# Activations at byte 112 and split weights at byte 176 of every 256, in a decoder trunk on one Trainium2 core

## The chip, the core and the metric

The kernel runs on one core of a Trainium2 chip. The metric is the device time in microseconds (us). Before the change, three timed runs took 594.8, 600.5 and 599.28 us; their median is 599.28 us. The profile is one further execution of the same program.

## What is computed

The reference is a decoder trunk with two layers over 256 tokens and 1024 features. The first layer has causal attention of 16 heads of 64 (one block of 256 keys, so the block selection is empty), the second a windowed attention whose keys and values come from 4 heads; both are followed by a gated feed-forward network with a causal convolution of width 3. Cut to what matters:

```python
for l in range(2):
    if l == 0:
        q, k, v = split(rmsnorm(x, attn_norm[0]) @ w_qkv_a[0], 3)    # 16 heads
        o = attention(rope(q), rope(k), v)                           # causal
    else:
        k, v = split(rmsnorm(x, kv_norm) @ w_kv_b, 2)                # 4 heads
        q = rmsnorm(x, attn_norm[1]) @ w_q_b[0]
        o = window_attention_with_sinks(rope(q), rope(k), v, sinks)  # 128 keys back
    x = x + o @ w_o[l]
    u = rmsnorm(x, ffn_norm[l]) @ w_up[l]                            # 1024 -> 5632
    u = conv_b + sum(conv_w[j] * shifted(u, 2 - j) for j in range(3))
    gate, val = split(u, 2)
    x = x + (silu(gate) * val) @ w_down[l]                           # 2816 -> 1024
out = rmsnorm(x, final_norm)
```

All of it is in float32. rope turns the first 16 features of each head.

## The kernel before

Every large product is made of three: an operand is split into a high part (rounded by a copy to fp32r, line 150 for the weights) and a low part (the difference, line 153), and high times high, high times low and low times high are summed in PSUM. The weights come in 101 units of 128 partitions x 2048 columns (1 MB), each loaded by SP into one of three buffers named wr, split by ScalarE into wh and by VectorE into wl (four buffers each), and used once. Activations lie feature by feature in tiles of 128 x 4 x 256 named q (function quad, line 75), 15 buffers of 4096 bytes a partition that all stages share; the same buffers hold the loaded input (x0), the unscaled activations y, the final gains fin_t and the last rows xf.

The stages run one after another on TensorE: projections and attention of layer 0 (to about 120 us), its up projection (line 575 to 577, to 251 us), its down projection (line 487 to 492), then the same for layer 1. In the up projection one unit is one block of 128 gate and 128 value features: 8 chunks of the 1024 inputs x 2 x 3 products = 48 matmuls, each with a 128 x 128 piece of wh or wl as the stationary operand and 256 columns of q as the moving one. In the down projection and in the projections of layer 0 it is the other way round: 128 x 128 of q are stationary, and 512 columns of wh or wl move. A matmul instruction shows in the profile as a weight load (PEld) and a matmul (PE); the weight load of the next matmul runs under the matmul before it.

The order on each engine is that of the program text: the function chain puts a step off until TensorE's estimated clock has gone on by so many nanoseconds, and require emits it earlier where its result is needed.

Where the tiles lie: the pools one, qd, wk and wp are laid out one after another, and each tile starts at the next multiple of 32 bytes. Of the tiles that matter, the built program has these starts, counted within 256 bytes: all q tiles at 32, all wr, wh and wl tiles at 96, the diagonal keys kd at 192, the identity and the residual xr at 32, the temporaries m2 at 160 and m3 at 96. A q tile is 4096 bytes long and a weight tile 8192, and each operand of a matmul starts a multiple of 512 bytes into its tile, so these numbers hold for every large matmul of the kernel, whichever buffer it uses.

rb (1024 bytes, made at line 885) holds the reciprocal norm of each token on all partitions; it is written and read in the two feed-forward stages only. The rotary step (rope, line 305) uses two temporaries ta and tb from the pool wk, one buffer each; the rotary tables are made at the start in tiles invf, pos_f, tri, arg and trig (lines 728 to 786).

Of the kernel before, what the change touches and what calls it, by code (L numbers as in the profile page):

```python
# [14 lines left out]
P = 128  # L15
# [22 lines left out]

# columns of the packed per-partition constants
G_ATTN0, G_KV, G_ATTN1 = 0, 8, 16  # L40
# [3 lines left out]

# weight units, in the order of their use
U_V0 = 0
# [14 lines left out]
def trunk(ctx: ExitStack, tc, x, xT, pos, cpk, fin, sinks, w, out):  # L61
# [9 lines left out]
    def nm(s):  # L71
        uid[0] += 1
        return f"{s}_{uid[0]}"

    def quad():
        return qd.tile([P, 4, S], F32R, tag="q", name=nm("q"))

# [17 lines left out]

# [1 line left out]
    # Instructions are issued in the order of emission. clock is the tensor engine's progress; what waits for another  # L97
    # engine is put off by an estimated latency, behind work that is ready by then.
    clock = [0.0]
# [17 lines left out]
    def chain(key, *steps, urgent=0):  # L117
        """steps: (delay after the step before, function)."""
        def run(k):
            if urgent:  # L120
                with tc.high_priority(offset=urgent):
                    steps[k][1]()
            else:
                steps[k][1]()
            if k + 1 < len(steps):
                put_off.append((clock[0] + steps[k + 1][0], key, lambda: run(k + 1)))
        put_off.append((clock[0] + steps[0][0], key, lambda: run(0)))

    def require(*key):
        """emit now what is put off under this key."""  # L130
        while True:
            mine = [t for t in put_off if t[1] == key]
            if not mine:
                return
            run_item(min(mine, key=lambda t: t[0]))

# [1 line left out]
    wq = {}  # L138
# [16 lines left out]
    def weights(i):  # L155
        wq[i] = (wp.tile([P, UNIT], F32R, tag="hi", name=f"wh{i}", bufs=4),
                 wp.tile([P, UNIT], F32R, tag="lo", name=f"wl{i}", bufs=4))

    def prepare(i):
        """split the weights of unit i, paced by the tensor engine."""  # L160
        if i >= N_UNITS:
# [19 lines left out]
    def used(i):  # L181
        """all products with unit i are emitted: its place is that of unit i + 4."""
        prepare(i + 4)
# [13 lines left out]

# [1 line left out]
    ident = one.tile([P, P], F32, name="ident")  # L199
# [10 lines left out]
    def warm_up(n):  # L210
        """products that nothing reads keep the tensor engine's clock up while the first loads are under way."""
        if n:
            t = bank("u")
            for _ in range(int(n)):
                nc.tensor.matmul(t[:, :P], ones, ones, start=True, stop=True)

# [1 line left out]
    sums = {}  # L218

    def new_hT():  # L220
        """feature-major activations: hi and lo, 8 chunks of [128, 256] in two tiles each."""
        return [(quad(), quad()) for _ in range(2)]

    def feats(b, n, sets, key, keep=None):
        """half n of the residual of token block b, times gains, to feature-major hi and lo parts."""
        ts = [bank("t"), bank("t")]
# [33 lines left out]
    def rstd_of(b):  # L260
        """rsqrt(mean(x^2) + eps) of the residual rows of token block b."""
        require("sq", b)
# [11 lines left out]
    def proj(o, hT, b, wv, units=()):  # L274
        """o[128 tokens of block b, n] = h @ W; wv(c) -> (hi, lo) of rows chunk c; units end with this block."""
        n = o.shape[-1]
# [28 lines left out]
    def rope(t, nh, b):  # L305
        """t: [128, nh, 64] in place."""
        ta = wk.tile([P, 8, ROT], F32, tag="ta", name=nm("ta"), bufs=1)[:, :nh]
        tb = wk.tile([P, 8, ROT], F32, tag="tb", name=nm("tb"), bufs=1)[:, :nh]
        c = cs[:, b].unsqueeze(1).to_broadcast([P, nh, ROT])
# [8 lines left out]
    def to_feature(t, n, b, hi, lo, key, then=None):  # L318
        """t: [128 tokens, n*128] -> hi, lo [128, n, tokens of block b]."""
        pt = bank("t")  # L320
# [14 lines left out]
    def rotate(o, n, b, hi, lo, key, copy, then=None):  # L335
        """projection o of token block b: copy(t) scales it out of PSUM, then rope and transpose to hi, lo."""
        t = mid()[:, :n * P]
        chain(key, (150.0, lambda: copy(t)),
              (750.0, lambda: rope(t.rearrange("p (h d) -> p h d", d=HD), 2 * n, b)),
              (1000.0, lambda: to_feature(t, n, b, hi, lo, key, then)))  # L340

    def attention(qk, ready, filler, lead, rate, msk, vcol, sink):
        """8 pairs of heads; qk[g] = (q hi, q lo, k hi, k lo, k chunk, diagonal k); filler: products that fill the waits."""
        oT = []
# [89 lines left out]
        def values(j, pT):  # L434
            """feature-major attention of a pair of heads, and its hi and lo parts."""
            require("pT", j)
# [31 lines left out]
    class Down:  # L468
        """residual += parts^T @ W, rows of 1024; two K chunks a unit; wait(i): parts of unit i are emitted."""

# [32 lines left out]
        def finish(self, i0, after, tail=None):  # L503
            """units from i0, so ordered that half of a token block is ready after each step."""
            last = self.n_u - 1
# [21 lines left out]
        def end(self, b, n, tail):  # L527
            """the last unit's products with one half of the columns, in two pieces of their own."""
            i = self.n_u - 1
# [26 lines left out]
    def ffn(layer, u_up, u_dn, hT, y, rb, after, tail=None):  # L556
# [23 lines left out]
        def scale_x(m):  # L580
            """chunks 2m and 2m + 1 of the activations times rstd, in parts, for the units from n_raw."""
            c = slice(2 * (m % 2), 2 * (m % 2) + 2)
# [73 lines left out]
    def row_bcast(rb, b):  # L656
        """rb[:, block b] = 1 / rms of each token, on all partitions."""
        r = rstd_of(b)
# [14 lines left out]

# [1 line left out]
    hT = new_hT()  # L675
    x0 = [qd.tile([P, 4, S], F32, tag="q", name=nm("x0")) for _ in range(2)]

# [48 lines left out]

    # rotary tables: cs = [cos cos], sn = [-sin sin] per token
    invf = one.tile([P, HALF], F32, name="invf")
    for j in range(HALF):
        nc.gpsimd.memset(invf[:, j:j + 1], float(THETA ** (-2.0 * j / ROT)))  # L730
    pos_f = one.tile([P, NB], F32, name="pos_f")
    nc.gpsimd.tensor_copy(pos_f, pos_i)
    tri = one.tile([P, 5, NB, HALF], F32, name="tri")
    ang, kk, kh, kl, rr = (tri[:, j] for j in range(5))
# [7 lines left out]
    for c in (TWO_PI_1, TWO_PI_2, TWO_PI_3):  # L742
        for k in (kh, kl):
            nc.gpsimd.tensor_scalar(out=kk, in0=k, scalar1=-c, scalar2=None, op0=ALU.mult)
            nc.gpsimd.tensor_tensor(out=rr, in0=kk, in1=src, op=ALU.add)
            src = rr
    arg = one.tile([P, 2, NB, HALF], F32, name="arg")
    nc.gpsimd.tensor_scalar(out=arg[:, 0], in0=rr, scalar1=PI_IN, scalar2=-PI_IN, op0=ALU.min, op1=ALU.max)
# [29 lines left out]
    nc.gpsimd.tensor_scalar(out=arg[:, 1], in0=kk, scalar1=-1.0, scalar2=HALF_PI, op0=ALU.mult, op1=ALU.add)  # L778
    trig = one.tile([P, 2, NB, HALF], F32, name="trig")
    nc.scalar.activation(trig, arg, AF.Sin)  # L780
# [32 lines left out]
    def spread(g, src, w):  # L813
        """keys of block 0 of two chunks to the diagonal: the heads of a pair side by side."""
        for e in range(2):
# [67 lines left out]
    hT = new_hT()  # L883
    y = [qd.tile([P, 4, S], F32, tag="q", name=nm("y")) for _ in range(2)]
    rb = one.tile([P, S], F32, name="rb")

# [18 lines left out]

# [1 line left out]
    kT = quad()  # L907
# [38 lines left out]
    hT = new_hT()  # L946
    y = [qd.tile([P, 4, S], F32, tag="q", name=nm("y")) for _ in range(2)]

# [7 lines left out]

    fin_t = qd.tile([P, D], F32, tag="q", name="fin_t")

    xf = [qd.tile([P, D], F32, tag="q", name=f"xf{b}") for b in range(NB)]

# [13 lines left out]
    def tail(m, o):  # L974
        """the last quarter rows of token block 1: residual, sum of squares, and after the last one the scaled rows."""
        st = sums[1]
# [31 lines left out]
def pack(inp):  # L1008
    """Weights as [unit, 128, 2048] in the order of use, rows of K on the partitions."""
    import numpy as np  # L1010
# [29 lines left out]
    halves(k_major(inp["w_kv_b"]))  # L1040
    # the heads of a pair belong to neighbouring key heads
    order = [(2 * (j // 4) + e) * 4 + j % 4 for j in range(NH // 2) for e in range(2)]
# [46 lines left out]
```

## Time and profile before

| | before |
|---|---|
| timed runs | 594.8, 600.5, 599.28 us |
| span of the profiled execution | 594.0 us |
| TensorE matmuls busy | 583.7 us (98%) |
| weight loads busy | 513.4 us (86%) |
| VectorE busy | 430.1 us (72%) |
| ScalarE busy | 382.4 us (64%) |
| GpSimd busy | 106.0 us (18%) |
| mean DMA rate | 170 GB/s |

The profile reads as follows. A busy share says how much of the span an engine had an instruction under way; matmuls are pipelined, so that one that is listed with 280 ns may start 113 ns after the one before it. How fast TensorE gets on is therefore read from the starts in the timeline, or from the number of matmuls in a stretch, and not from the length of one.

### The profile page before, as it was taken

The page shows a single profiled execution, that of the slowest core. Times are in us where ns is not written, and L with a number is a line of the kernel's source. Part 1 is how long each engine was busy: PE and PEld are TensorE (multiplying, and loading weights), DVE is VectorE, ACT ScalarE, POOL GpSimd, SP SyncE. Part 2 cuts the span into 40 slices and gives each one's busy share as a digit, 9 for nine tenths or more (in the row PEclk, how much of TensorE's full clock was granted, in tenths as well). Part 3 has the DMA queues.
Part 4 walks back from the last instruction along what each step waited for, and adds up shares of the span by engine and source line. Part 5 has one row for each costly group of instructions (what it writes and reads, how often), then busy time and mean ns, then how long its engine had stood idle before and what let it go on. Part 6 is the DMA issues. An engine that isn't in the chain of part 4 may idle for free.

```text
span 594.0 us, 10194 instructions
## 1 busy us (share of the span) xinstructions
PE 583.7 (98%) x3858; PEld 513.4 (86%) x3858; DVE 430.1 (72%) x927; ACT 382.4 (64%) x769; POOL 106.0 (18%) x124
## 2 busy tenths in 40 slices
PE   7999999999999999999999999999999999999995
PEld 6877777789999999988878977679999999988884
DVE  4597668589977777776369778769987677777714
ACT  5788767578566565656349688757865565656513
POOL 6321101001222323220001100000222223232003
PEclk9999999999999999999999999999999999999999
DMA  7963534314554444548542622233273545445701
GB/s 237 394 247 128 213 142 142 142 38 177 213 189 167 182 173 163 193 151 333 191 175 83 273 72 72 72 142 137 90 271 143 204 151 189 168 168 222 284 0 71
DMA packets 17184, 101.00 MB, mean 170 GB/s; under 512 B 2288, under 2 KB 2672, under 8 KB 5744
## 3 DMA queue, kind: packets, MB, share of 16 engines
q1 hardware_dynamic: 16992, 100.09, 45.4%
q8 instruction: 30, 0.49, 0.3%
q10 hardware_dynamic: 144, 0.26, 0.1%
q14 instruction: 18, 0.15, 0.1%
HBM read 99.30 MB, written 1.05 MB: 169 GB/s over the span
## 4 chain that ended last, share of the span: by engine, by line
PE 72%; DVE 9%; ACT 7%; POOL 4%; issue 4%; DMA 2%; SPq 0%; POOLq 0%; DVEq 0%; ACTq 0%
PE acc L487 9%; PE acc L488 9%; PE acc L492 9%; POOL m L619 4%; PE acc L281 4%; PE acc L282 4%; PE acc L283 4%; PE u L575 4%; PE u L576 3%; PE u L577 3%; PE t L575 3%; PE t L576 3%; PE t L577 3%; PE t L441 3%; DVE wl L153 2%
## 5 line engine op out<-in xcount | busy, mean ns | idle before, releaser
L153 DVE TENSOR_TENSOR wl<-wr,wh 128x1024 fp32r<-128x1024 f32 (+1 forms) x208 | 224.7, 1100 | 42.2 <-ACT wh L150 41.8
L150 ACT ACTIVATE wh<-wr 128x1024 fp32r<-128x1024 f32 (+1 forms) x208 | 192.7, 956 | 41.8 <-PE acc L492 26.9
L619 POOL TENSOR_TENSOR m<-m,m 128x256 f32<-128x256 f32 x44 | 67.1, 1527 | 205.9 <-DVE m L614 177.6
L487 PE MATMUL acc<-wh,q 128*128 128x512 f32 x238 | 96.2, 404 | 0.0
L488 PE MATMUL acc<-wl,q 128*128 128x512 f32 x238 | 94.8, 398 | 0.0
L575 PE MATMUL u<-q,wh 128*128 128x256 f32 x320 | 89.5, 281 | 0.0
L576 PE MATMUL u<-q,wh 128*128 128x256 f32 x320 | 89.1, 279 | 0.0
L577 PE MATMUL u<-q,wl 128*128 128x256 f32 x320 | 89.1, 279 | 0.0
L575 PE MATMUL t<-q,wh 128*128 128x256 f32 x288 | 80.4, 279 | 0.2 <-DVE m L614 0.2
L492 PE MATMUL acc<-wh,q 128*128 128x512 f32 x238 | 80.4, 399 | 0.0
L577 PE MATMUL t<-q,wl 128*128 128x256 f32 x288 | 80.3, 279 | 0.0
L576 PE MATMUL t<-q,wh 128*128 128x256 f32 x288 | 80.3, 279 | 0.0
L623 ACT ACTIVATE q<-m 128x256 fp32r<-128x256 f32 x44 | 18.4, 417 | 82.0 <-POOL m L619 82.0
L575 PEld LDWEIGHTS u<-q,wh 128*128 128x128 f32 x320 | 60.5, 190 | 0.1
L577 PEld LDWEIGHTS u<-q,wl 128*128 128x128 f32 x320 | 60.2, 188 | 0.0
L576 PEld LDWEIGHTS u<-q,wh 128*128 128x128 f32 x320 | 60.1, 188 | 0.0
L281 PE MATMUL acc<-wh,q 128*128 128x512 f32 (+1 forms) x160 | 57.7, 361 | 0.0
L282 PE MATMUL acc<-wl,q 128*128 128x512 f32 (+1 forms) x160 | 56.4, 353 | 0.1
L283 PE MATMUL acc<-wh,q 128*128 128x512 f32 (+1 forms) x160 | 56.2, 351 | 0.0
L575 PEld LDWEIGHTS t<-q,wh 128*128 128x128 f32 x288 | 54.7, 190 | 0.3 <-issue 0.3
L576 PEld LDWEIGHTS t<-q,wh 128*128 128x128 f32 x288 | 54.1, 188 | 0.0
L577 PEld LDWEIGHTS t<-q,wl 128*128 128x128 f32 x288 | 54.1, 188 | 0.0
(150 smaller groups left out, 1029.3 us busy)
## 6 DMA issues: line engine op xcount, KB each, us to landing
wr<-in_w SPq DMA_DIRECT2D x89, 1024.0 KB, 4.8
wr<-in_w SPq DMA_DIRECT2D x12, 256.0 KB, 5.6
xr<-in_x SPq DMA_DIRECT2D x4, 256.0 KB, 7.4
x<-in_xT SPq DMA_DIRECT2D x3, 256.0 KB, 6.2
out<-m SPq DMA_DIRECT2D x3, 256.0 KB, 2.3
fin_t<-in_fin SPq DMA_DIRECT2D x1, 512.0 KB, 5.7
x<-in_xT SPq DMA_DIRECT2D x2, 128.0 KB, 2.7
out<-m ACTq DMA_DIRECT2D x1, 256.0 KB, 2.0
```

The lines of the kernel that those rows point to most:

```text
L150: nc.scalar.activation(wq[i][0][:, c], raws[i][:, c], AF.Copy)
L153: nc.vector.tensor_tensor(out=wq[i][1][:, c], in0=raws[i][:, c], in1=f(wq[i][0][:, c]), op=ALU.subtract)
L281: nc.tensor.matmul(o, xh[:, blk(b)], wh, start=(c == 0), stop=False)
L282: nc.tensor.matmul(o, xh[:, blk(b)], wl, start=False, stop=False)
L283: nc.tensor.matmul(o, xl[:, blk(b)], wh, start=False, stop=(c == KC - 1))
L487: nc.tensor.matmul(o, ph[:, blk(b)], hi[:, s_], start=first, stop=False)
L488: nc.tensor.matmul(o, ph[:, blk(b)], lo[:, s_], start=False, stop=False)
L492: nc.tensor.matmul(o, pl[:, blk(b)], hi[:, s_], start=False, stop=end)
L575: nc.tensor.matmul(o, hi[:, s_], xh, start=(c == 0), stop=False)
L576: nc.tensor.matmul(o, hi[:, s_], xl, start=False, stop=False)
L577: nc.tensor.matmul(o, lo[:, s_], xh, start=False, stop=(c == KC - 1))
L619: nc.gpsimd.tensor_tensor(out=h, in0=gs, in1=t[1], op=ALU.mult)
```

## The change

Three things are edited; no instruction is added or removed, and on each engine the instructions stand in the same order as before, with the same operands but for the renamed temporaries. One rotary multiplication on VectorE loses a wait for GpSimd.

- A helper spaced takes a tile 64 floats (256 bytes) longer than needed and returns the part that starts 4 floats (16 bytes) in. All q tiles, wh and wl are taken through it. A tile of 48 floats named pad is put into the pool one.
- So that there is room, rb is made at the start and the rotary temporaries ta and tb and the tables invf, pos_f, tri, arg and trig become slices of it.
- Comments and text strings of functions are taken out, which moves line numbers by up to 8.

In the built program the starts within 256 bytes become: q 112 (tile at 96, plus 16), wh and wl 176 (tile at 160, plus 16), wr 160, kd 0, the identity 224, xr 32, m2 224, m3 160. The distance from q to the weights is 64 bytes before and after; both move on by 80 bytes. All starts named before were multiples of 32; now q, wh and wl are 16 past one. The tiles' pitch becomes 4352 and 8448 bytes.

```diff
@@ -72,8 +72,15 @@
-    def quad():
-        return qd.tile([P, 4, S], F32R, tag="q", name=nm("q"))
+    SKIP, ROUND = 4, 64
+
+    def spaced(pool, n, dt, tag, name, bufs):
+        return pool.tile([P, n + ROUND], dt, tag=tag, name=name, bufs=bufs)[:, SKIP:SKIP + n]
+
+    def quad(dt=F32R, name="q"):
+        return spaced(qd, 4 * S, dt, "q", nm(name), 15).rearrange("p (c t) -> p c t", c=4)
...
     def weights(i):
-        wq[i] = (wp.tile([P, UNIT], F32R, tag="hi", name=f"wh{i}", bufs=4),
-                 wp.tile([P, UNIT], F32R, tag="lo", name=f"wl{i}", bufs=4))
+        wq[i] = (spaced(wp, UNIT, F32R, "hi", f"wh{i}", 4),
+                 spaced(wp, UNIT, F32R, "lo", f"wl{i}", 4))
...
     xr = [one.tile([P, D], F32, name=f"xr{b}") for b in range(NB)]
 
-    # ---- constants ---------------------------------------------------------
+    rb = one.tile([P, S], F32, name="rb")
+    one.tile([P, 48], F32, name="pad")
...
     def rope(t, nh, b):
-        """t: [128, nh, 64] in place."""
-        ta = wk.tile([P, 8, ROT], F32, tag="ta", name=nm("ta"), bufs=1)[:, :nh]
-        tb = wk.tile([P, 8, ROT], F32, tag="tb", name=nm("tb"), bufs=1)[:, :nh]
+
+        ta, tb = (rb[:, k * P:(k + 1) * P].rearrange("p (h d) -> p h d", d=ROT)[:, :nh] for k in range(2))
...
-    x0 = [qd.tile([P, 4, S], F32, tag="q", name=nm("x0")) for _ in range(2)]
+    x0 = [quad(F32, "x0") for _ in range(2)]
...
-    invf = one.tile([P, HALF], F32, name="invf")
+    invf = rb[:, 144:152]
...
-    pos_f = one.tile([P, NB], F32, name="pos_f")
+    pos_f = rb[:, 152:154]
...
-    tri = one.tile([P, 5, NB, HALF], F32, name="tri")
+    tri = rb[:, :80].rearrange("p (k b d) -> p k b d", k=5, b=NB)
...
-    arg = one.tile([P, 2, NB, HALF], F32, name="arg")
+    arg = rb[:, 80:112].rearrange("p (k b d) -> p k b d", k=2, b=NB)
...
-    trig = one.tile([P, 2, NB, HALF], F32, name="trig")
+    trig = rb[:, 112:144].rearrange("p (k b d) -> p k b d", k=2, b=NB)
...
     hT = new_hT()
-    y = [qd.tile([P, 4, S], F32, tag="q", name=nm("y")) for _ in range(2)]
-    rb = one.tile([P, S], F32, name="rb")
+    y = [quad(F32, "y") for _ in range(2)]
...
-    fin_t = qd.tile([P, D], F32, tag="q", name="fin_t")
-
-    xf = [qd.tile([P, D], F32, tag="q", name=f"xf{b}") for b in range(NB)]
+    fin_t = spaced(qd, D, F32, "q", "fin_t", 15)
+
+    xf = [spaced(qd, D, F32, "q", f"xf{b}", 15) for b in range(NB)]
```

## Rows read from the trace of the kernel before

**Rows 1.** The page: busy time by engine; busy tenths in 40 slices, granted clock.

```profile
PE 583.7 (98%) x3858; PEld 513.4 (86%) x3858; DVE 430.1 (72%) x927; ACT 382.4 (64%) x769; POOL 106.0 (18%) x124
...
PE   7999999999999999999999999999999999999995
...
PEclk9999999999999999999999999999999999999999
```

**Rows 2.** The page: share of the chain that ended last, by engine.

```profile
PE 72%; DVE 9%; ACT 7%; POOL 4%; issue 4%; DMA 2%; SPq 0%; POOLq 0%; DVEq 0%; ACTq 0%
```

**Rows 3.** TensorE in stretches: length, busy (x matmuls), clock, DMA share, GB/s.

```profile
133.00:251.00 118.00, 118.00 (x1004) 1.00 0.49 184
251.00:307.00 56.00, 56.00 (x243) 1.00 0.58 213
...
413.00:514.00 101.00, 101.00 (x894) 1.00 0.47 180
514.00:527.00 13.00, 12.85 (x106) 1.00 0.48 166
527.00:584.00 57.00, 57.00 (x246) 1.00 0.42 156
```

**Rows 4.** Starts in up projection, layer 0, 48 matmuls apart: start us, length, line.

```profile
200.26 0.28 PE L575 MATMUL t<-q,wh 128*128 128x256 f32 x1
...
205.92 0.28 PE L575 MATMUL u<-q,wh 128*128 128x256 f32 x1
```

**Rows 5.** The same in the up projection of layer 1, 48 matmuls apart.

```profile
460.01 0.28 PE L575 MATMUL u<-q,wh 128*128 128x256 f32 x1
...
465.45 0.28 PE L575 MATMUL t<-q,wh 128*128 128x256 f32 x1
```

**Rows 6.** The same, down projection of layer 0, 512 columns, 24 matmuls apart.

```profile
270.05 0.40 PE L488 MATMUL acc<-wl,q 128*128 128x512 f32 x1
...
275.65 0.40 PE L488 MATMUL acc<-wl,q 128*128 128x512 f32 x1
```

**Rows 7.** The same, output projection of layer 1, 512 columns, 21 matmuls apart.

```profile
392.10 0.39 PE L492 MATMUL acc<-wh,q 128*128 128x512 f32 x1
...
396.90 0.39 PE L492 MATMUL acc<-wh,q 128*128 128x512 f32 x1
```

**Rows 8.** All engines around 514 us: where the distance of the starts changes.

```profile
514.30 0.28 PE L577 MATMUL t<-q,wl 128*128 128x256 f32 x1
514.36 0.19 PEld L575 LDWEIGHTS u<-q,wh 128*128 128x128 f32 x1
...
514.42 0.33 PE L575 MATMUL u<-q,wh 128*128 128x256 f32 x1
```

**Rows 9.** Score products whose moving operand is kd, layer 0.

```profile
40.60 0.28 PE L365 MATMUL u<-kd,q 128*128 128x256 f32 x1
40.72 0.28 PE L366 MATMUL u<-kd,q 128*128 128x256 f32 x1
40.84 0.28 PE L367 MATMUL u<-kd,q 128*128 128x256 f32 x1
```

**Rows 10.** Six transposes whose stationary operand is m3.

```profile
93.38 0.82 PE L420 MATMUL t<-ident,m 128*128 128x128 f32 x6
```

**Rows 11.** Four transposes whose stationary operand is m2.

```profile
56.99 0.60 PE L322 MATMUL t<-ident,m 128*128 128x128 f32 x4
```

**Rows 12.** Four transposes whose stationary operand is xr.

```profile
307.85 0.60 PE L228 MATMUL t<-ident,xr 128*128 128x128 f32 x4
```

**Rows 13.** Groups by line: form, count | busy us, mean ns | idle before, releaser.

```profile
L612 DVE SCALAR_TENSOR_TENSOR m<-u,cp,m 128x255 f32<-128x255 f32 x36 | 17.2, 478 | 7.8 <-ACT m L608 7.8
...
L614 DVE SCALAR_TENSOR_TENSOR m<-u,cp,m 128x254 f32<-128x254 f32 x36 | 17.2, 479 | 0.6
```

**Rows 14.** Loads of x0: time from issue to landing.

```profile
DMA to landing us min/median/max: 2.7/5.8/6.6
```

**Rows 15.** Rotary multiplications on VectorE from 35 to 120 us, by form.

```profile
L310 DVE TENSOR_TENSOR ta<-m,cs 128x128 f32<-128x128 f32 x6 | 1.7, 282 | 1.9 <-ACT m L839 1.9
```

More of the change, by code (lines that the diff above doesn't have):

```diff
@@ L946, in trunk @@
     hT = new_hT()
-    y = [qd.tile([P, 4, S], F32, tag="q", name=nm("y")) for _ in range(2)]
+    y = [quad(F32, "y") for _ in range(2)]
     def after_b(b, n):
```

## Prediction, made before the changed kernel was run

> **What bounds the kernel now.** I read the page first: TensorE has matmuls under way for 583.7 of 594.0 us, at the full granted clock from end to end [rows 1], and makes up 72% of the chain that ended last [rows 2]. Then I read TensorE by stretches [rows 3]: in both up projections and both down projections it is busy for the whole stretch, 118.00 of 118.00 us and so on. So nothing is gained there by a wait that gets shorter; only the distance from one matmul to the next counts, and that I read from the starts.
>
> The reader is to see that this distance takes several values for the same instruction. In the up projection of layer 0, 48 matmuls of 256 columns take 205.92 - 200.26 = 5.66 us, 117.9 ns each [rows 4]; in that of layer 1 they take 465.45 - 460.01 = 5.44 us, 113.3 ns each [rows 5]. With 512 columns moving it is 5.60 / 24 = 233.3 ns in the down projection [rows 6] and 4.80 / 21 = 228.6 ns in the output projection of layer 1 [rows 7]. At 2.4 GHz and one column a cycle it would be 106.7 and 213.3 ns, so between 6% and 11% are lost inside the matmul stream. The two values are steady for a hundred microseconds: 1004 matmuls in 118 us, then 894 in 101 us [rows 3]. They are not a matter of the clock, which is 1.00 in both [rows 3]. And they flip at a disturbance: at 514.36 us a weight load starts 0.06 us after the matmul before it, the next matmul has 0.33 us instead of 0.28 [rows 8], and from there the stretch runs slow: 106 matmuls in 13 us [rows 3]. I call the two values the fast and the slow lock: the weight load of the next matmul and the moving columns of this one read the same memory at the same time and settle into one of two rhythms.
>
> **The change part by part.** No instruction is added, removed or moved, so the sum has no row of its own; what can change is what an instruction costs at its new address.
>
> Matmul operands: q from 32 to 112, weights from 96 to 176, the tiles' pitch by 256. This is the only term that lies on the path. The trace cannot price it, since each large product has one pair of starts in it. Both ends come from the distances above. Upper end of a gain: the loss vanishes. The stretches of [rows 3] then shrink by 1 - 106.7/117.9 = 9.5% of 118 and 13 us (12.4 us), 1 - 106.7/113.3 = 5.8% of 101 us (5.9 us) and 1 - 213.3/233.3 = 8.6% of 56 and 57 us (9.7 us), in all 28 us. Upper end of a loss: each large matmul pays the difference between the locks once more, 4.6 ns for the 44 x 48 = 2112 of the up projections and 4.7 ns for the 30 x 24 = 720 of the down and output projections, 13 us, beside the fast stretch turned slow (101 us x 0.041 = 4.1 us). Between them I take the fast lock everywhere: a rhythm that the hardware holds by itself for 101 us with the old starts, which a new offset of the two read streams can make the usual one. It gives 1 - 113.3/117.9 = 3.9% of 118 + 13 us, 5.1 us, and 1 - 228.6/233.3 = 2.0% of 56 + 57 us, 2.3 us: together 7.4 us.
>
> VectorE and ScalarE at new starts: 0. The nearest rows are two multiplications that write 4 and 8 bytes into their tile and take 478 and 479 ns, 36 of each kind [rows 13], so a start off 32 bytes shows no price there. What hides a price: both engines are busy for 72% and 64% [rows 1], and TensorE waited for neither in the up projections [rows 3]. If that cover were gone, the split of the weights would be late next.
>
> The loads of x0 now land 16 bytes past a multiple of 32: priced at 0. They take 2.7 to 6.6 us each [rows 14]; the price lies between 0 and one median landing again, 5.8 us, and a gain is excluded because the first weights share the queue.
>
> The rotary temporaries in rb: 0. rb is free while rotary steps run, since it is written after the last one of layer 0 and again after the last one of layer 1; the multiplication keeps its 282 ns [rows 15]. One wait for GpSimd goes; it had been met. If the sharing did make rb late, one rotary multiplication, 0.3 us, would stand ahead of the norms.
>
> Sum: 594.0 - 7.4 = 586.6 us of span. The fastest timed run, 594.8 us, lies 0.8 us over the span of the profile; I take that as what lies around it and come to **587.4 us**. The median, 599.28 us, lies 5.3 us over the profiled span. A profiled execution in which layer 1 ran slow too would have 594.0 + 4.1 + 0.8 = 598.9 us, so I read the spread of the three runs as the lock falling one way or the other. Against the median the forecast is 2.0% less.
>
> **The rivals.** A: the address does not decide, and the lock goes on falling as stalls have it. For this: transposes with the stationary operand at three different starts follow each other at the same distance, four in 0.60 us with m2 at 160 and with xr at 32, six in 0.82 us with m3 at 96, which is 0.11 us each by the difference [rows 10, 11, 12]. Products with kd at 192 as the moving operand start 0.12 us apart like those with q at 32 [rows 9]. And the flip at 514 us came with no change of address. Against it: the transposes move 128 columns only, the kd products come in threes, and no operand of a matmul has stood 16 past a multiple of 32 so far. The time stays between 594.8 (layer 1 fast) and 598.9 us (both slow).
>
> The Trainium skill speaks for A: "SBUF — State Buffer", section "Who interferes with whom", gives TensorE two read ports of its own and says "PE and ACT never wait on anyone", by which the new starts change nothing and the time is that of A. The trace bears out the result of [rows 9 to 12], but two steady distances at one set of addresses show that something in the two read streams does wait.
>
> B: slower. Each matmul whose operands start in the middle of a 32-byte piece fetches one piece more. For it speaks that the loss grows with the columns moved, 6.6 ns over the ideal at 256 [rows 5] and 15.3 ns at 512 [rows 7], as a cost of fetching would. Against it: the cost would come once for an operand, and the loss seen is not of that kind. Price: both locks slow and the upper end of a loss, 598.9 + 13 = 612 us. It decides from 605.3 us, that is from 6.4 us over 2832 large matmuls, 2.3 ns each.
>
> C: the loss nearly vanishes: 594.0 - 28 + 0.8 = 567 us. For it: every start of before was a multiple of 32 and every one had a loss, so the loss may belong to that. Against it: nothing in the trace runs without it.
>
> The Trainium skill, "TensorE: Matmul & The Clock Gate", section "Back-to-back issue gap", gives columns / 2.4 + 2.5 ns for a warm matmul, 109.2 and 215.8 ns; an estimate with these in place of the ideal takes about 22 us off in place of 28. The trace does not agree: 113.3 and 228.6 ns are the least that it holds.
>
> **How the numbers follow.** About 1% is what a measurement of this kernel can tell from no change, 593.3 to 605.3 us around the median. Fast lock everywhere: 0.37, 584 to 592 us. A: 0.34, 595 to 599 us. B: 0.15, 600 to 612 us. C, wholly or in part: 0.14, 560 to 580 us. Faster therefore has 0.37 + 0.14 = 0.51, the same 0.34, slower 0.15. The prediction is the likeliest, 587.4 us, with 584 to 592 us as its own range. The range over all cases is 565 to 604 us: it leaves out about a third of C and most of B, some 0.2.
>
> **What would show it.** Right: starts 113.3 ns apart in both up projections, starts 229 ns apart or less in both down projections, and little spread between runs. A: the same two distances as now, in either layer by chance. B: distances over 117.9 and 233.3 ns. C: under 113.3 ns and well under 228.6 ns. The forecast is wrong if the distances stay and the time moves, which would point to the loads at the start or to VectorE.

## The result, and the profile of the changed kernel

Four runs of the changed kernel took 588.82, 589.42, 588.27 and 588.18 us, median 588.55; four of the kernel before took 594.8, 600.5, 599.28 and 595.9 us, median 597.59. The ratio is 0.9885, interval 0.984 to 0.993, that is 1.2% less; the two medians lie 9.0 us or 1.5% apart. The change makes the kernel 1 to 1.5% faster. The slowest run after is 5.4 us faster than the fastest of these runs before, and the spread of the runs fell from 5.7 to 1.2 us. Runs of the kernel before that were taken later, beside the experiments, reach from 591.42 to 600.50 us, so against its best run the gain is 3 us and against its slowest 12.

The page of the profiled execution (588.82 us, span 586.8 us): busy time by engine, TensorE's busy tenths in 40 slices, the granted clock, and the chain that ended last by engine.

```profile
PE 575.4 (98%) x3858; PEld 507.7 (87%) x3858; DVE 430.4 (73%) x927; ACT 383.2 (65%) x769; POOL 106.9 (18%) x124
...
PE   8999999999999999999999999999999999999995
...
PEclk9999999999999999999999999999999999999998
...
PE 59%; DVE 15%; ACT 9%; POOL 7%; issue 5%; DMA 2%; SPq 1%; POOLq 0%; DVEq 0%; ACTq 0%
```

Against [rows 1, 2], TensorE is still busy 98% of a span that is 7.2 us shorter, and the clock is as full as before. VectorE, ScalarE and GpSimd do the same work in about the same time. What is new is in the chain: TensorE's share fell from 72 to 59%, and VectorE's rose from 9 to 15%. TensorE is quicker now, and the work around it ends last more often.

Lines 584 to 586 are 575 to 577 of before, line 496 is 487: these line numbers moved by 9. TensorE by stretches, the answer to [rows 3]: length, busy time and matmuls in it, clock, DMA share, GB/s.

```profile
127.00:247.00 120.00, 119.60 (x1052) 1.00 0.50 176
251.00:302.00 51.00, 51.00 (x227) 1.00 0.64 234
400.00:520.00 120.00, 119.61 (x1052) 1.00 0.49 176
526.00:579.00 53.00, 53.00 (x236) 1.00 0.41 149
```

Both up projections now hold 1052 matmuls in 120 us. They read the same, where [rows 3] had 1004 in 118 us in layer 0 and 894 in 101 us in layer 1. The busy time is 119.60 of 120.00 us: something else holds TensorE up there for 0.4 us, where [rows 3] had 0.15 us in layer 1 and nothing in layer 0.

The starts in the up projection of layer 0, 48 matmuls apart (compare [rows 4]):

```profile
200.12 0.28 PE L584 MATMUL t<-q,wh 128*128 128x256 f32 x1
...
205.56 0.28 PE L584 MATMUL u<-q,wh 128*128 128x256 f32 x1
```

The same in layer 1, 48 apart (compare [rows 5]):

```profile
460.05 0.28 PE L584 MATMUL t<-q,wh 128*128 128x256 f32 x1
...
465.49 0.28 PE L584 MATMUL u<-q,wh 128*128 128x256 f32 x1
```

And in the down projection of layer 0, 512 columns, 24 apart (compare [rows 6]):

```profile
266.35 0.39 PE L496 MATMUL acc<-wh,q 128*128 128x512 f32 x1
...
271.79 0.39 PE L496 MATMUL acc<-wh,q 128*128 128x512 f32 x1
```

All three take 5.44 us: 113.3 ns for a matmul of 256 columns in both layers, and 5.44 / 24 = 226.7 ns for one of 512. The slow distances of [rows 4] (117.9 ns) and [rows 6] (233.3 ns) are gone. No instruction is shorter for another reason: the split of the weights keeps its 1101 ns on VectorE (1100 before) and 959 ns on ScalarE (956 before).

Stage by stage, from the first start of one to the first start of the next, the 7.2 us of span lie here:

| stretch | before, us | after, us | difference |
|---|---|---|---|
| start and attention of layer 0 | 126.15 | 125.81 | -0.3 |
| up projection, layer 0 | 125.00 | 121.49 | -3.5 |
| down projection of layer 0, attention of layer 1 | 153.47 | 151.69 | -1.8 |
| up projection, layer 1 | 121.55 | 121.49 | -0.1 |
| down projection of layer 1, to the end of the span | 67.8 | 66.3 | -1.5 |

### The profile page after: what moved, and what is told of

It reads as the page before. It is cut to its first block, busy times and chain, and to the rows that moved or that the text cites. A ratio compares the mean times of both kernels' runs of the same rounds, so it can differ in the third digit from the quotient of the medians.

```text
span 586.8 us, 10194 instructions
## 1 busy us (share of the span) xinstructions
PE 575.4 (98%) x3858; PEld 507.7 (87%) x3858; DVE 430.4 (73%) x927; ACT 383.2 (65%) x769; POOL 106.9 (18%) x124
## 4 chain that ended last, share of the span: by engine, by line
PE 59%; DVE 15%; ACT 9%; POOL 7%; issue 5%; DMA 2%; SPq 1%; POOLq 0%; DVEq 0%; ACTq 0%
PE acc L496 9%; PE acc L501 9%; PE acc L497 9%; POOL m L628 6%; DVE m L623 4%; PE acc L291 4%; ACT m L617 4%; DVE m L621 4%; DVE wl L160 4%; PE acc L292 4%; PE acc L293 4%; PE t L450 3%; DMA wr<-in_w 2%; PE t L429 2%; ACT wh L157 2%
## 5 line engine op out<-in xcount | busy, mean ns | idle before, releaser
L160 DVE TENSOR_TENSOR wl<-wr,wh 128x1024 fp32r<-128x1024 f32 (+1 forms) x208 | 224.8, 1101 | 36.7 <-ACT wh L157 36.3
L496 PE MATMUL acc<-wh,q 128*128 128x512 f32 x238 | 94.4, 397 | 0.0
L497 PE MATMUL acc<-wl,q 128*128 128x512 f32 x238 | 93.0, 391 | 0.0
L584 PE MATMUL u<-q,wh 128*128 128x256 f32 x320 | 88.5, 277 | 0.1
L585 PE MATMUL u<-q,wh 128*128 128x256 f32 x320 | 88.0, 275 | 0.0
L584 PE MATMUL t<-q,wh 128*128 128x256 f32 x288 | 79.4, 276 | 0.7 <-DVE m L623 0.7
L585 PE MATMUL t<-q,wh 128*128 128x256 f32 x288 | 79.2, 275 | 0.0
L501 PE MATMUL acc<-wh,q 128*128 128x512 f32 x238 | 79.0, 392 | 0.0
```

Source lines behind the costliest of these rows:

```text
L160: nc.vector.tensor_tensor(out=wq[i][1][:, c], in0=raws[i][:, c], in1=f(wq[i][0][:, c]), op=ALU.subtract)
L496: nc.tensor.matmul(o, ph[:, blk(b)], hi[:, s_], start=first, stop=False)
L497: nc.tensor.matmul(o, ph[:, blk(b)], lo[:, s_], start=False, stop=False)
L501: nc.tensor.matmul(o, pl[:, blk(b)], hi[:, s_], start=False, stop=end)
L584: nc.tensor.matmul(o, hi[:, s_], xh, start=(c == 0), stop=False)
L585: nc.tensor.matmul(o, hi[:, s_], xl, start=False, stop=False)
```

## The experiments

The theory after the result: the starts of the two operands of a matmul decide whether TensorE keeps the fast distance, and the new starts make it the only one. Rivals: the longer tiles or the moved temporaries do it; one operand's start alone does it; what counts is the place within the 256 bytes; what counts is only the distance between activations (q) and weights (w), or only that they start off a multiple of 32. The kernels are the changed one with other skips. In the first the helper gets a skip for the weights of its own, which all others keep:

```diff
-    SKIP, ROUND = 4, 64
+    SKIP, SKIP_W, ROUND = 0, 0, 64
...
-        return pool.tile([P, n + ROUND], dt, tag=tag, name=name, bufs=bufs)[:, SKIP:SKIP + n]
+        skip = SKIP if tag == "q" else SKIP_W
+        return pool.tile([P, n + ROUND], dt, tag=tag, name=name, bufs=bufs)[:, skip:skip + n]
```

A skip counts floats, so it moves a start by four times as many bytes from 96 (q) and 160 (w). The table holds all kernels: starts within 256 bytes, the distance from q to w, the mean distance of the starts in the up (256 columns) and down projections (512 columns) of layer 0 and 1 in the profiled run, without the matmuls behind which TensorE waited, and the timed runs.

| kernel | q, w | apart | 256 columns, ns | 512 columns, ns | runs, us: median (range, count) |
|---|---|---|---|---|---|
| before | 32, 96 | 64 | 117.6, 113.9 | 233.2, 233.3 | 597.59 (594.80 to 600.50, 4) |
| after | 112, 176 | 64 | 113.5, 113.5 | 226.8, 226.7 | 588.55 (588.18 to 589.42, 4) |
| e1 | 96, 160 | 64 | 113.6, 113.6 | 229.1, 229.0 | 592.65 (589.84 to 595.79, 4) |
| e2 | 32, 96 | 64 | 117.6, 117.6 | 233.1, 233.3 | 599.44 (598.02 to 600.29, 10) |
| e3 | 112, 160 | 48 | 119.2, 119.2 | 231.9, 231.9 | 602.38 (601.86 to 602.79, 8) |
| e4 | 96, 176 | 80 | 118.8, 118.8 | 231.1, 231.1 | 600.90 (600.24 to 602.06, 10) |
| e5 | 48, 112 | 64 | 113.5, 113.5 | 226.8, 226.7 | 588.27 (587.62 to 588.92, 4) |
| e6 | 144, 208 | 64 | 113.5, 113.5 | 226.8, 226.7 | 587.98 (587.43 to 588.70, 4) |
| e7 | 104, 168 | 64 | 120.8, 120.8 | 239.8, 240.0 | 611.30 (610.80 to 611.44, 4) |
| e8 | 112, 240 | 128 | 120.0, 120.0 | 233.3, 233.3 | 605.57 (605.32 to 606.53, 4) |
| e9 | 112, 112 | 0 | 118.3, 118.3 | 231.2, 233.3 | 600.68 (600.13 to 601.23, 2) |
| e10 | 112, 144 | 32 | 120.0, 120.0 | 232.3, 232.2 | 604.03 (603.85 to 604.21, 2) |
| e11 | 112, 208 | 96 | 117.8, 117.8 | 233.3, 233.3 | 600.83 (600.26 to 601.39, 2) |
| e12 | 112, 48 | 192 | 118.3, 118.3 | 229.0, 228.9 | 593.55 (589.90 to 598.22, 8) |

The kernel before ran beside each group: beside e1 to e4 its median was 599.37 us (23 runs, 6 of them from 593.75 to 596.17 and 17 from 598.75 to 600.50), beside e5 to e8 595.45 (7 runs), beside e9 to e12 595.13 (9 runs, 591.42 to 598.96). It moves by up to 7.5 us within one group, more than the 4.4 us that one up projection gains from the fast distance, so ratios of different groups don't compare. The three groups ran on three different chips, and no other kernel ran in two of them. On which chip the runs in the first two rows of the table were made is not recorded. So times are compared within a group first; the distances compare throughout.

The fences below show TensorE in two stretches that lie inside the up and the down projection of layer 0, from 140 to 240 and from 260 to 300 us, columns as above. The changed kernel has 882 and 178 matmuls there:

```profile
140.00:240.00 100.00, 99.95 (x882) 1.00 0.51 180
...
260.00:300.00 40.00, 40.00 (x178) 1.00 0.70 263
```

The kernel before has 852 and 173:

```profile
140.00:240.00 100.00, 100.00 (x852) 1.00 0.48 180
...
260.00:300.00 40.00, 40.00 (x173) 1.00 0.64 237
```

### e1: no skip at all (96, 160)

The diff is the one above.

> The changed kernel with the 16 bytes left out: q starts at 96 and the split weights at 160 within 256 bytes, both multiples of 32, 64 bytes apart as always; longer tiles, shared rotary temporaries and everything else as in the changed kernel. Theory (the 16 bytes past a multiple of 32 hold the fast lock): slow distances come back, 117.8 ns in parts of the up projections and 229 to 233 ns in the down projections, 594 to 601 us. Rival P (it is the place within 256 bytes or the longer tiles): the distances of the changed kernel, 113.3 and 226.7 ns, about 588 us. Rival A (the lock falls by chance of the stalls): anything between 588 and 601 us, mixed within a kind of matmul.

Ratio 0.9896, interval 0.985 to 0.9942.

```profile
140.00:240.00 100.00, 100.00 (x883) 1.00 0.50 180
...
260.00:300.00 40.00, 40.00 (x177) 1.00 0.70 262
```

The profiled run had the fast distance in both up projections (883 in 100 us) and a middle one of 229 ns in the down projections, made of 226, 229 and 232 ns in turn. The profiled run is the fastest; the others took up to 6 us longer and have no trace. The expectation of the theory, 594 to 601 us, was missed: three of the four runs are faster than that. I read the spread as distances that fall one way or the other, as before, and the 16 bytes as what makes them steady; the runs show the spread, not the distances behind it.

### e2: the old starts in the longer tiles (32, 96)

```diff
-    SKIP, ROUND = 4, 64
+    SKIP, SKIP_W, ROUND = 48, 48, 64
```

> The changed kernel with the tiles' parts starting 192 bytes in, in place of 16: q starts at 32 and the split weights at 96 within 256 bytes, as before the change; the longer tiles and the shared rotary temporaries stay. Theory: as before the change, 594 to 601 us, with 117.8 ns in at least one up projection or 233 ns in the down projections. Rival R (the rest of the change, longer tiles or the rotary tile, made the gain): about 588 us with 113.3 and 226.7 ns.

Ratio 1.0015, interval 0.9992 to 1.0038.

```profile
140.00:240.00 100.00, 100.00 (x852) 1.00 0.50 180
...
260.00:300.00 40.00, 40.00 (x173) 1.00 0.64 237
```

852 and 173 matmuls, the counts of the kernel before. All the rest of the change (longer tiles, another order of tiles, the rotary temporaries in rb) is still in this kernel, and it gains nothing. All ten runs lie where the slow distance puts both layers. They are also all slower than every run of e1 (598.02 us and more against 595.79 and less), although both kernels have multiples of 32, 64 apart, and ran on one chip: among such starts the place within the 256 bytes does count. Whether the longer tiles have a part in that, when the kernel before got away from it in some runs, was not followed.

### e3 and e4: the 16 bytes for one operand only

e3, for q alone (112, 160):

```diff
-    SKIP, ROUND = 4, 64
+    SKIP, SKIP_W, ROUND = 4, 0, 64
```

> The changed kernel with the 16 bytes on the activations alone: q at 112, the split weights at 160. Moving operand in the up projections is q, in the down projections the weights. If the moving operand's start decides: up projections 113.3 ns, down projections 229 to 233 ns, about 590 to 592 us. If the stationary operand's start decides: up projections partly 117.8 ns, down projections 226.7 ns, 590 to 597 us. If both have to be 16 past: slow in both, 594 to 601 us. If the distance between the two decides: no one value is expected.

Ratio 1.0061, interval 1.0033 to 1.0088.

```profile
140.00:240.00 100.00, 100.00 (x841) 1.00 0.50 179
...
260.00:300.00 40.00, 40.00 (x174) 1.00 0.64 233
```

e4, for the weights alone (96, 176):

```diff
-    SKIP, ROUND = 4, 64
+    SKIP, SKIP_W, ROUND = 0, 4, 64
```

> The mirror of the run with the activations alone: q at 96, the split weights at 176. If the moving operand's start decides: up projections partly 117.8 ns, down projections 226.7 ns, 590 to 597 us. If the stationary operand's start decides: up projections 113.3 ns, down projections 229 to 233 ns, about 590 to 592 us. If both have to be 16 past: 594 to 601 us.

Ratio 1.0041, interval 1.0016 to 1.0066.

```profile
140.00:240.00 100.00, 100.00 (x844) 1.00 0.50 179
...
260.00:300.00 40.00, 40.00 (x175) 1.00 0.65 237
```

Each half is slower than no skip at all, by 8 to 10 us against e1, and in all runs: 841 and 844 matmuls in 100 us. Neither operand's start works by itself. With e1 and the changed kernel these two make a square. q at 96 is fast with the weights at 160 (113.6 ns) and slow with them at 176 (118.8 ns); q at 112 is slow at 160 (119.2 ns) and fast at 176 (113.5 ns). So neither start has a price of its own: the price hangs on the pair. These are the distances of the profiled runs; by the times, every run of e1 is faster than every run of e3 and e4. The times lie at and just above the 594 to 601 us that were expected if both have to be 16 past. Whether it is the distance of 64 alone, or the 16 bytes as well, e5 to e12 are to tell.

### e5 and e6: other places, 64 apart, 16 past a multiple of 32

e5, the old starts plus 16 (48, 112):

```diff
-    SKIP, ROUND = 4, 64
+    SKIP, SKIP_W, ROUND = 52, 52, 64
```

> The changed kernel with the parts starting 208 bytes in: q at 48 and the split weights at 112 within 256 bytes, that is the starts of the kernel before plus 16, 64 bytes apart. Theory (both operands 16 past a multiple of 32, their distance a multiple of 32): steady 113.3 and 226.7 ns in all four projections of the feed-forward stages, about 588 us and runs within 1 us of each other. Rival P (the place within 256 bytes decides, 96 to 112 being better than 32 to 48): distances between those, 590 to 600 us, runs that differ by several us.

Ratio 0.9851, interval 0.9805 to 0.9898.

```profile
140.00:240.00 100.00, 100.00 (x884) 1.00 0.52 180
...
260.00:300.00 40.00, 40.00 (x178) 1.00 0.70 261
```

e6, 32 further than the changed kernel (144, 208):

```diff
-    SKIP, ROUND = 4, 64
+    SKIP, SKIP_W, ROUND = 12, 12, 64
```

> The changed kernel with 48 bytes in place of 16: q at 144, the split weights at 208, both 16 past a multiple of 32 but also 16 past a multiple of 64 (112 and 176 are 48 past one). Theory: steady 113.3 and 226.7 ns, about 588 us. Rival P64 (48 past a multiple of 64 is what counts): other distances, 590 to 601 us.

Ratio 0.9847, interval 0.98 to 0.9894.

```profile
140.00:240.00 100.00, 100.00 (x884) 1.00 0.50 180
...
260.00:300.00 40.00, 40.00 (x178) 1.00 0.72 262
```

884 and 178 matmuls each, the same two distances as in the changed kernel, in both layers. Among these three pairs, both 16 past and 64 apart, the place within the 256 bytes does not matter. e2 and e5 differ in 16 bytes for both operands and in nothing else of the program: 117.6 against 113.5 ns, and 11.2 us between the medians. They ran on different chips; on the chip of e5 the kernel before, which has the starts of e2, took 594.48 to 599.60 us and e5 587.62 to 588.92. The two are 0.3 and 0.6 us faster than the changed kernel, which is less than the spread of its runs; I count none of them as better.

### e7: 8 bytes in place of 16 (104, 168)

```diff
-    SKIP, ROUND = 4, 64
+    SKIP, SKIP_W, ROUND = 2, 2, 64
```

> The changed kernel with 8 bytes in place of 16: q at 104, the split weights at 168, both 8 past a multiple of 32 and of 16. If whole 16-byte pieces count, an operand of 1024 bytes now spans one piece more: slower than without any skip, over 593 us, with distances above 113.3 and 226.7 ns. If only an offset from the multiple of 32 counts, whatever its size: about 588 us, 113.3 and 226.7 ns.

Ratio 1.0238, interval 1.018 to 1.0295.

```profile
140.00:240.00 100.00, 100.00 (x830) 1.00 0.50 178
...
260.00:300.00 40.00, 40.00 (x168) 1.00 0.57 211
```

830 and 168 matmuls: 120.8 and 240 ns, the slowest kernel of all, and steady in both layers. "Off a multiple of 32" is not what helps; a start 8 past costs. The price is near that of the prediction's rival B, 611.3 us against 612. The number agrees; whether a piece more is fetched, as B has it, no run shows.

### e8 to e11: 16 past a multiple of 32, other distances

e8, 128 apart (112, 240):

```diff
-    SKIP, ROUND = 4, 64
+    SKIP, SKIP_W, ROUND = 4, 20, 64
```

> The changed kernel with q at 112 as it is and the split weights at 240, 128 bytes apart in place of 64, both 16 past a multiple of 32. Theory: steady 113.3 and 226.7 ns, about 588 us. Rival D (the distance of 64 counts beside the 16 bytes): irregular or slower distances, as in the two runs with distances of 48 and 80, 594 to 603 us.

Ratio 1.0144, interval 1.0096 to 1.0192.

```profile
140.00:240.00 100.00, 100.00 (x836) 1.00 0.50 179
...
260.00:300.00 40.00, 40.00 (x173) 1.00 0.61 225
```

e9, the same start for both (112, 112):

```diff
-    SKIP, ROUND = 4, 64
+    SKIP, SKIP_W, ROUND = 4, 52, 64
```

> q at 112 as in the changed kernel, the split weights also at 112: 0 bytes apart within 256. Theory D (the distance decides how the weight load and the moving columns settle; 64 is one that settles fast): other distances than 113.3 and 226.7 ns, 595 to 610 us. Rival (128 alone is bad, any other distance that is a multiple of 32 settles fast): about 588 us.

Ratio 1.0124, interval 1.0012 to 1.0236.

```profile
140.00:240.00 100.00, 100.00 (x847) 1.00 0.50 178
...
260.00:300.00 40.00, 40.00 (x174) 1.00 0.65 237
```

e10, 32 apart (112, 144):

```diff
-    SKIP, ROUND = 4, 64
+    SKIP, SKIP_W, ROUND = 4, 60, 64
```

> q at 112, the split weights at 144: 32 bytes apart within 256. Theory D: other distances than 113.3 and 226.7 ns, 595 to 610 us. Rival: about 588 us.

Ratio 1.018, interval 1.007 to 1.0291.

```profile
140.00:240.00 100.00, 100.00 (x836) 1.00 0.50 179
...
260.00:300.00 40.00, 40.00 (x174) 1.00 0.64 231
```

e11, 96 apart (112, 208):

```diff
-    SKIP, ROUND = 4, 64
+    SKIP, SKIP_W, ROUND = 4, 12, 64
```

> q at 112, the split weights at 208: 96 bytes apart within 256. Theory D: other distances than 113.3 and 226.7 ns, 595 to 610 us. Rival: about 588 us.

Ratio 1.0126, interval 1.0014 to 1.0238.

```profile
140.00:240.00 100.00, 100.00 (x851) 1.00 0.50 179
...
260.00:300.00 40.00, 40.00 (x174) 1.00 0.65 237
```

In all four both starts are 16 past a multiple of 32, as in the changed kernel, and q stands where it stands there. All four are 12 to 17 us slower than the changed kernel (e8 17 us slower than e5 and e6 on its own chip), with 117.8 to 120.0 ns in the up and 231 to 233 ns in the down projections. That ended the idea that any distance of a multiple of 32 would do: the distance between the two operands counts as well. For e8 rival D was right in kind and its 594 to 603 us too low.

### e12: 64 apart the other way round (112, 48)

```diff
-    SKIP, ROUND = 4, 64
+    SKIP, SKIP_W, ROUND = 4, 36, 64
```

> q at 112, the split weights at 48, 192 bytes on (64 the other way) within 256. Theory D with a sign: 595 to 610 us; theory D without a sign (only how far they are apart): 113.3 and 226.7 ns, about 588 us.

Ratio 0.9965, interval 0.9917 to 1.0012. The eight runs took 598.22, 593.47, 593.62, 597.84, 590.25, 589.90, 593.33 and 593.85 us; the profiled one is the first, with 118.3 ns in the up projections and 229 ns in the down projections:

```profile
140.00:240.00 100.00, 100.00 (x847) 1.00 0.50 180
...
260.00:300.00 40.00, 40.00 (x177) 1.00 0.64 237
```

Both expectations missed: the times are neither steadily 588 us nor 595 to 610. The spread of 8 us is like that of the kernel before and of e1, which I read in the same way; the faster runs have no trace. With the weights 64 below q, both 16 past, the kernel is not steadily fast.

### What stands

Of the starts tried, three pairs give the fast distance over whole stages in the profiled run, and times within 1.3 us in all runs: 48 and 112, 112 and 176, 144 and 208. They have in common that both are 16 past a multiple of 32 and that the weights start 64 bytes above q. Take away the first (before, e1) and the distance is fast in some profiled stages; move by 8 (e7) and it is the slowest; take away the second (e8 to e11) and it is fast in no profiled stage.

Two rivals can be settled from the traces. One is that other engines or DMAs get in the way of TensorE, and more so at some starts. I took each distance in the down projections together with the 100 ns before it, and kept those in which no instruction of VectorE, ScalarE or GpSimd ran and no DMA packet was under way. In the kernel before 63 such distances have a mean of 233.4 ns, in the changed kernel 59 have 226.7, in e7 87 have 240.0: the values of the table. So the price is there when nothing but TensorE is at work. Together with the square of e1, e3, e4 and the changed kernel this points to the two reads of TensorE, of the weights and of the moving columns, getting in each other's way.

The other is that starts modulo 512 count. The pitches of 4352 and 8448 bytes are 17 and 33 times 256, so in all kernels but the one before neighbouring buffers start 256 bytes apart modulo 512, and in the changed kernel 18 of the 22 units of each up projection still have 113.3 ns each (the first two and the last two hold waits or other work).

Why 16 and 64 are the numbers is not shown by any run: the trace gives starts of matmuls, not the reads behind them. Single tiles with a place of their own were not tried.

## Why the prediction came out right, point by point

**The time.** Forecast 587.4 us with 584 to 592 as its own range, measured 588.55. By the ratio the gain is 1.2%, with an interval from 0.7 to 1.6%; e5 and e6, which have the same distances, put it at 1.5%. The forecast gain of 2.0% was against the median of three runs. The likeliest case, the fast distance everywhere, is what happened in the feed-forward stages; the prediction gave it a chance of 0.37.

**The cause, right only in part.** The prediction said that a new offset of the two read streams could make the fast distance the usual one, while by the section on the change their distance is 64 bytes before and after. The step was argued and half wrong: the distance has to stay 64 (e8 to e11), and what made the rhythm steady is that both starts went 16 past a multiple of 32 (e2 against e5, e1 against the changed kernel). Nothing in the trace of before could have told 16 from 8, whose price is +23 us (e7 against the changed kernel). That the start chosen was one of the good ones is in part luck. The picture behind the two distances, the two reads of TensorE settling into a rhythm, was argued; the square and the stretches without other engines support it, and no run shows the reads.

**The up projections: 5.1 us forecast, 4.9 found.** In each stage 1055 distances can be read. Layer 0 went from a mean of 117.64 to 113.46 ns, 4.4 us; layer 1 from 113.93 to 113.47, 0.5 us, the end that [rows 8] showed as flipped.

**The down projections: 2.3 us forecast, 3.4 found.** This term was mis-sized. The step took the 228.6 ns of the output projection [rows 7] as the fast distance for 512 columns. The fast one is 226.7 ns; 229 ns is a middle rhythm, which e1 holds for a whole stage. 264 and 258 matmuls times 6.4 and 6.6 ns are 1.7 + 1.7 us.

**Not in the sum at all: the projections of the attention stages, 1.2 us.** Their 512-column matmuls went from 229.7 to 227.6 ns in layer 0 (384 of them, 0.8 us), and those of layer 1 by 1.7 ns, with a little from its 256-column ones (0.4 us together). The prediction took its stretches from [rows 3], and the attention stages have none there.

**Given back: 2.2 us, priced at nothing.** These gains make 9.5 us, and the span fell by 7.2. The time that TensorE waited between two large matmuls rose by about 1.9 us, 1.3 of it in the up projections (1.2 to 2.5 us in both), and 0.2 us lie behind the last matmul. The clearest place is at the end of the up projection of layer 0, where the profile shows an idle TensorE. Timeline of all engines:

```profile
241.11 0.48 DVE L623 SCALAR_TENSOR_TENSOR m<-t,cp,m 128x254 f32<-128x254 f32 x1
241.12 0.28 PE L586 MATMUL u<-q,wl 128*128 128x256 f32 x1
...
241.71 0.19 PEld L584 LDWEIGHTS t<-q,wh 128*128 128x128 f32 x1 [0.52 <-ACT wh L157]
241.74 0.36 PE L584 MATMUL t<-q,wh 128*128 128x256 f32 x1 [0.35 <-DVE m L623]
```

The matmul of line 586 starts at 241.12, the next one 0.62 us later. The profile puts the weight load down to ScalarE and the matmul to VectorE; VectorE's line 623, which reads the PSUM tile t that the matmul is to write, ends at 241.11 + 0.48 = 241.59 us, 0.12 us ahead of the weight load, and is the one that fits in time; no run took that wait away. So with 48 matmuls in 5.44 us in place of 5.66 TensorE comes to a PSUM tile before VectorE has done with it. Such waits are counted by line:

```profile
PE t L584 <- DVE m L623: 0.7, 2, 0.3
```

There are two of 0.3 us on that line in place of one of 0.2 us before. The prediction wrote that what hides a price here was that TensorE waited for neither engine in the up projections [rows 3]; it did not go on to ask whether that holds for a quicker TensorE.

**Around the span: 0.8 us forecast, 2.0 found.** The step set the fastest of three timed runs against the span of another execution. The profiled run's own time is 588.82 us with a span of 586.8. With 2.0 us the sum would have given 588.6 us. The forecast span, 586.6 us, is within 0.2 us of the measured one, because 9.5 us in place of 7.4 and 2.2 us given back in place of none nearly cancel. That the sum came so near is luck: two of its terms were wrong, and their errors cancel.

**The spread.** The reading of the 5.7 us between the runs of before as an up projection that falls into one distance or the other fits, but only one of these runs has a trace. For it: 23 runs beside e1 to e4 lie in two groups some 4 to 5 us apart, as 1055 x 4.2 ns = 4.4 us would have it, and the changed kernel, e5, e6 and e7 stay within 1.3 us. Not foreseen: beside e9 to e12 three of nine runs of before took 591.42 to 592.59 us, below the 594.8 us that the prediction had as the lower end of A. Two fast up projections would make such a time; no trace of one was kept.

**The rivals.** A, that the address does not decide, is out as a rule: e1 to e12 differ from the changed kernel in start addresses only, and their medians span 23 us, as do those of e6 and e7 on one chip. At some pairs of starts it holds: the trace of before has both distances at (32, 96). The Trainium skill spoke for it ("SBUF — State Buffer", section "Who interferes with whom", PE among those that never wait); as to other engines the traces agree: without any of them at work e7 keeps its 240.0 ns and the changed kernel its 226.7 ("What stands"). For the starts of TensorE's own operands the measurement decides against that reading, since one and the same instruction follows the last after 113.3 or 120.8 ns by its operands' starts, at a granted clock of 1.00 in every row of stretches above. B, a piece more to fetch for starts inside a 32-byte piece, is out for 16 bytes and gives the time of e7 for 8. C, that the loss nearly vanishes, is out: no kernel holds less than 113.3 and 226.7 ns over a stage, so the 109.2 and 215.8 ns that the Trainium skill gives ("TensorE: Matmul & The Clock Gate", section "Back-to-back issue gap") are not met over a stage in any run here. That section gives them for a matmul by itself and for a stream of weight loads and matmuls about 131 ns at 512 columns, which is further still from the 226.7 ns measured.

**The zeros.** VectorE at starts off 32 bytes: line 621 and 623 still take 478 and 479 ns [rows 13], and the split of the weights 1101 ns. Rotary steps: 282 ns as in [rows 15]. The loads of the input: a median of 5.7 us for the three of 256 KB (6.2 before), and the up projection of layer 0 starts 0.3 us earlier, not later. e2 tests all of them but the new starts together: no gain that can be measured, and a loss of 0.4% at most by its interval.

## What to carry to other kernels

When TensorE is busy all the time, read the distance of matmul starts, stage by stage, before anything else. Two steady values for one instruction were the sign here that the addresses of its two operands left something to gain, and a spread between runs of the same size went with them. What helped here was to move both operands by 16 bytes and keep their distance of 64; whether it helps a kernel with other operands is not shown, so try several pairs and measure. The loss from a wrong start (23 us here at 8 bytes) is larger than the gain from the right one. A quicker TensorE uses up the slack of whoever frees its PSUM tiles, so ask before the sum what each wait that is now met would be at the new pace.

## What the hardware showed that was not expected

- One matmul has, at different starts of its operands, at least five mean distances, each kept over whole stages: 113.3, 117.8, 118.3, 120.0 and 120.8 ns for 256 columns, 226.7, 229, 231 to 233.3 and 240 ns for 512. All at a granted clock of 1.00. At (32, 96) it has two of them, 113.3 and 117.8 ns.
- Neither operand's start has a price of its own: in the profiled runs (96, 160) and (112, 176) have 113.6 and 113.5 ns, (96, 176) and (112, 160) 118.8 and 119.2. The price stays when VectorE, ScalarE, GpSimd and the DMA queues are idle (240.0 ns in e7, 226.7 in the changed kernel).
- The least ones are 272 and 544 cycles at 2.4 GHz (113.3 x 2.4, 226.7 x 2.4), that is 17 for every 16 columns; 120.0 and 240 ns are 18 for every 16. No large matmul got under 17 in 16 over a stage.
- A start 8 bytes past a multiple of 32 costs 6 to 7% of each large matmul against one that is 16 past: 7.4 of 113.3 ns, and 13.3 of 226.7.
- The distance between the operands is not symmetric: with both 16 past a multiple of 32, weights 64 bytes above q are steadily fast, weights 64 bytes below q (e12) are not.
